# Two transformer blocks in float32 on one core: the low halves of the weights prepared first and multiplied last, and four smaller edits

## The chip, the core and the metric

The kernel runs on one core of a Trainium2 chip. The core has a matrix engine (TensorE, "PE" in the profile, with its weight loads as "PEld"), a vector engine (DVE), a scalar engine (ACT), GpSimd (POOL) and SyncE (SP). Each engine works through its own instructions in their fixed order and waits on semaphores; transfers are issued by SP, ACT or POOL and run on 16 DMA engines. The metric is the device time of one execution in microseconds (us). The three runs shown took 2757.64, 2758.91 and 2762.56 us, so the median is 2758.91 us; the profiled execution took 2760.67 us.

## The reference

Two networks of two layers each run one after the other over 512 tokens of width 1024, all in float32. A layer of the first one, cut to what matters here:

```
h = rmsnorm(x, g_mix)
dq, dk, dv, c_q, c_kv_kr, xq, gate_logits = split(h @ w_in)
y_diff = diff_attention(dq, dk, dv, ...) @ w_diff_o      # 8 heads, two softmax maps a head
y_mla  = latent_attention(c_q, c_kv_kr, ...) @ w_mla_o   # 8 heads
mem_n  = rmsnorm(mem, mem_gain)
y_mem  = memory_cross_attention(xq, mem_n, w_mem_kv) @ w_cross_o   # 4 heads, 256 memory rows
merged = gates[0]*y_diff + gates[1]*y_mla + gates[2]*y_mem
x = x + merged @ w_out
x = x + square(relu(rmsnorm(x, g_mlp) @ w_mlp1)) @ w_mlp2
```

In `diff_attention` a head's output is `o = softmax0 @ v - lam * softmax1 @ v`, and then `o = rmsnorm(o, out_gain)` times a constant. A layer of the second network projects with `w_in_2`, mixes by four branches (two of them causal attention), and adds the product with `w_out_2`.

## The kernel before, in words

Activations lie in SBUF with features or tokens on the 128 partitions and 512 (or 256) columns beside them. A float32 product is made from three products of a shorter format: every operand is split into a high half (rounded to `float32r`) and a low half (the rest), and `mm3` (line 206) adds high x high, high x low and low x high in PSUM. For weights, `W[0]` (tile `whi`) is the high half and `W[1]` (tile `wlo`) the low one.

Weights stream through a ring. `load` (line 120) takes one unit's weights, mostly 128 x 2048 values (1 MB): SP fetches them from HBM into `wraw`, then the halves are made. `whi`, `wlo` and `wraw` have two buffers each. For the first two loads the low half is a subtraction. For all later ones ACT casts `whi` (line 135, pieces of 1216 and 832 columns), ACT writes the negated raw weights into `wlo` (line 144), and POOL issues a transfer (line 147) that adds `wraw` onto `wlo` as it moves.

The work is cut into units, each with a generator that issues its products in parts. `run` (line 176) goes through the list `ops`; when a unit is begun, the load of the next unit is recorded. That load needs the `whi` and `wlo` buffers of the unit before, so its casts can begin when PE has read that unit's last weights. From the order of recording, the tile framework makes a fixed order for each engine.

`proj_tok` (line 477) makes a tile of tokens (activations stationary, weights moving), `proj_feat` (line 484) a tile of features (weights stationary). Both call `mm3` for k = 0 to 7, so high and low products alternate. An MLP unit (`w1`, `w2`, lines 1348 and 1370) is two feature tiles of 24 products of 512 columns.

`diff_chain` (line 642) is one head of the differential attention: `T` transposes q and k, `soft` makes both softmax maps of a block of queries and joins them, `pt` transposes the probabilities, `AV` multiplies by v, `sums` adds squares over features on PE (`tok_sums`, line 435) and takes 1/sqrt (`rsqrt`, line 221: two integer steps and three Newton rounds of three, 11 small operations of DVE), and `fin` spreads the root by a copy on DVE and four transposes on PE (`bcast`, line 447; line 453), and scales the output. `mla_chain` (line 930) does the same for the latent attention. `cross` (line 986) makes the memory's keys (`kk`, line 1024) and values (`vv`) in four units of 48 products of 256 columns. `layer1` (line 1171) weaves chains and units.

Of the kernel before, what the change touches and what calls it, by code (L numbers as in the profile page):

```python
# [20 lines left out]
TB = 4  # L21
# [63 lines left out]
class Net:  # L85
# [34 lines left out]
    def load(self, spec):  # L120
# [12 lines left out]
        for a in range(0, sz, 1216):  # L133
            b = min(a + 1216, sz)
            nc.scalar.copy(hi[:, a:b], raw[:, a:b])  # L135
        if self.loaded < 2:
            e, step = (nc.gpsimd, 576) if eng == "pool" else (nc.vector, 768)
            for a in range(0, sz, step):
                b = min(a + step, sz)
                e.tensor_tensor(lo[:, a:b], raw[:, a:b], hi[:, a:b].bitcast(F32), op=OP.subtract)  # L140
        else:
            for a in range(0, sz, 1216):
                b = min(a + 1216, sz)
                nc.scalar.activation(lo[:, a:b], raw[:, a:b], AF.Copy, scale=-1.0)  # L144
            for a in range(0, sz, 2048):
                b = min(a + 2048, sz)
                nc.gpsimd.dma_start(lo[:, a:b].bitcast(F32), raw[:, a:b], accum_op=OP.add)  # L147
        self.loaded += 1
# [72 lines left out]
    def rsqrt(self, t, shape, name):  # L221
        v = self.nc.vector
# [11 lines left out]
    def setup_x(self, gain):  # L234
# [12 lines left out]
        self.xt, self.gm = xt, gm  # L247
        self.consts = b.tile([128, NCONST], F32, name="consts")
# [186 lines left out]
    def tok_sums(self, sq, scale, name, more=()):  # L435
# [8 lines left out]
        nc.vector.tensor_scalar(t_, ps[:, 0:8:2], scale, EPS, op0=OP.mult, op1=OP.add)  # L444
# [32 lines left out]
    def proj_tok(self, out, W, tb, c0, c1, lh=None, ll=None):  # L477
        lh, ll = lh or self.hh, ll or self.hl
        n = len(lh)
        sl = slice(tb * 128, tb * 128 + 128)  # L480
        for k in range(n):
            self.mm3(out, lh[k][:, sl], ll[k][:, sl], W[0][:, k, c0:c1], W[1][:, k, c0:c1], k == 0, k == n - 1)

    def proj_feat(self, out, W, c0, rh, rl, order=None, m=128):
        n = len(rh)
        for i, k in enumerate(order or range(n)):
            self.mm3(out, W[0][:, k, c0:c0 + m], W[1][:, k, c0:c0 + m], rh[k], rl[k], i == 0, i == n - 1)
            if i == n // 2 - 1 and n == 8:
                yield
# [152 lines left out]
    def diff_chain(self, l, h):  # L642
        X = {}

        def T():
            p = self.pool("diff")
            t1s, X["f"] = self.t1s.pop(h)
            for i, nm in enumerate(("q", "k")):
                ps = self.P("tq")
                for tb in range(TB):  # L650
                    c = (tb % 2) * 256 + i * 128
                    self.nc.tensor.transpose(ps[:, tb * 128:(tb + 1) * 128], t1s[tb // 2][:, c:c + 128], self.ident)
                hi = p.tile([128, 512], F32R, name=nm + "h", bufs=1)
                lo = p.tile([128, 512], F32R, name=nm + "l", bufs=1)
                self.split(hi, lo, ps)
                X[nm] = (hi, lo)

        def soft(qb):
# [3 lines left out]
            sm = self.sm([128, 2], "dsm")  # L662
# [14 lines left out]
            rs = self.sm([128, 2], "drs")  # L677
            nc.vector.reciprocal(rs, sm)
            c = self.sm([128, 1], "dc")
            nc.vector.tensor_tensor(c, rs[:, 1:2], self.neglam[:, l:l + 1], op=OP.mult)  # L680
            nc.vector.tensor_scalar(Ss[0][:, :n], Ss[0][:, :n], rs[:, 0:1], None, op0=OP.mult)
# [17 lines left out]
        def sums():  # L699
            t = self.tok_sums(X["sq"], 1.0 / 128, "oss")  # L700
# [9 lines left out]
        return T, [lambda qb=qb: soft(qb) for qb in range(4)], [lambda qb=qb: pt(qb) for qb in range(4)], [AV, sums, fin]  # L710
# [219 lines left out]
    def mla_chain(self, l, h):  # L930
        X = {}

        def T():
            p = self.pool("mla2")
            for nm, src, g in (("k", self.kt, self.gqk_mla[l][0:96]), ("q", self.qt, None)):
                ps = self.P("tq")
# [1149 lines left out]
```

## Time and profile before

| what | us |
|---|---|
| median of the three runs | 2758.91 |
| profiled execution | 2760.67 |
| its span, first to last instruction | 2758.8 |
| PE busy in it | 2613.7 (95%) |
| ACT busy | 1560.8 (57%) |
| DVE busy | 1375.5 (50%) |
| POOL busy | 363.8 (13%) |

PE is the busy engine. "Busy" is the union of the records of an engine; records of neighbouring matmuls overlap, so the pace of PE is read from start to start. Idle time of PE, 145.1 us of the span, is what waits put there. The profile names for each wait what ended it, and the mean granted clock of PE (0.976 here) in parts of 2.4 GHz.

### The profile page before, as it was taken

What the parts mean: (1) busy time and instruction counts of PE and PEld (TensorE: products, weight loads), DVE (VectorE), ACT (ScalarE), POOL (GpSimd) and SP (SyncE); (2) the same over time, 40 slices, a digit from 0 to 9 for tenths busy, and PEclk for the clock granted to TensorE, in tenths of its full rate; (3) what the DMA queues carried; (4) which work ended last, traced back from release to release, by engine and by line L of the source; (5) the groups of instructions that cost most, each with busy time, mean ns of one, the idle gap of its engine ahead of it and who ended that gap; (6) DMA issues with size and microseconds to landing.
All of it is one profiled execution on the core that took longest, in us unless ns stands there. A gap on an engine that the chain in (4) does not pass through costs nothing.

```text
span 2758.8 us, 37849 instructions
## 1 busy us (share of the span) xinstructions
PE 2613.7 (95%) x14168; PEld 2199.3 (80%) x14168; DVE 1375.5 (50%) x4128; ACT 1560.8 (57%) x2699; POOL 363.8 (13%) x396
## 2 busy tenths in 40 slices
PE   7999998899999999999999799899999999999997
PEld 7998787787777778998788787677777978788776
DVE  6876575333201213777567342211113489728894
ACT  5666676454544445566667454444445557656683
POOL 1000200001100122000110000100031212121111
PEclk8999999899999999999999899999999999999999
DMA  6554745668777778555564666777777764475543
GB/s 194 123 134 100 176 119 128 160 157 211 177 177 185 184 180 210 138 133 121 123 151 108 168 168 164 191 180 183 187 180 203 176 138 111 119 184 120 146 108 99
DMA packets 261208, 428.83 MB, mean 155 GB/s; under 512 B 21724, under 2 KB 217120, under 8 KB 237728
## 3 DMA queue, kind: packets, MB, share of 16 engines
q0 software_dynamic: 29088, 199.14, 36.0%
q1 hardware_dynamic: 231224, 226.90, 26.8%
q8 instruction: 112, 1.84, 0.3%
q14 instruction: 72, 0.59, 0.1%
q10 hardware_dynamic: 712, 0.36, 0.0%
HBM read 216.76 MB, written 10.49 MB: 82 GB/s over the span
## 4 chain that ended last, share of the span: by engine, by line
PE 68%; DMA 14%; issue 7%; ACT 6%; DVE 5%; POOL 0%; SPq 0%; POOLq 0%; DVEq 0%; ACTq 0%
PE mm L210 18%; PE mm L208 18%; PE mm L209 18%; DMA wlo<-wraw 11%; PE tp L616 2%; PE sc L609 2%; ACT whi L135 2%; DMA wraw<-in_w_in 2%; PE av L632 1%; ACT wlo L144 1%; DMA wraw<-in_w_mem_kv 1%; PE sc L441 1%; PE av L208 1%; PE sc L210 1%; PE sc L208 1%
## 5 line engine op out<-in xcount | busy, mean ns | idle before, releaser
L135 ACT CAST whi<-wraw 128x1216 fp32r<-128x1216 f32 (+4 forms) x380 | 393.9, 1056 | 455.9 <-PE mm L209 390.5
L210 PE MATMUL mm<-hh,wlo 128*128 128x512 f32 x1312 | 526.4, 401 | 28.0 <-DMA wlo<-wraw 26.1
L208 PE MATMUL mm<-hh,whi 128*128 128x512 f32 x1312 | 528.3, 403 | 6.0 <-ACT hh L1999 4.6
L209 PE MATMUL mm<-hl,whi 128*128 128x512 f32 x1312 | 524.5, 400 | 0.0
L144 ACT ACTIVATE wlo<-wraw 128x1216 fp32r<-128x1216 f32 (+4 forms) x376 | 392.2, 1064 | 103.2 <-PE mm L209 66.3
L147 POOL DMA_DIRECT2D wlo<-wraw x202 | 176.4, 886 | 1970.1 <-ACT wlo L144 1610.4
L208 PE MATMUL mm<-whi,hh 128*128 128x256 f32 (+4 forms) x1184 | 349.2, 295 | 9.6 <-DVE xm L308 7.2
L209 PE MATMUL mm<-wlo,hh 128*128 128x256 f32 (+4 forms) x1184 | 343.6, 291 | 14.0 <-DMA wlo<-wraw 13.9
L210 PE MATMUL mm<-whi,hl 128*128 128x256 f32 (+4 forms) x1184 | 341.8, 289 | 0.0
L210 PEld LDWEIGHTS mm<-hh,wlo 128*128 128x128 f32 x1312 | 249.4, 190 | 93.5 <-issue 16.2
L208 PEld LDWEIGHTS mm<-hh,whi 128*128 128x128 f32 x1312 | 249.6, 190 | 59.5 <-ACT hh L1999 7.4
L209 PEld LDWEIGHTS mm<-hl,whi 128*128 128x128 f32 x1312 | 249.9, 190 | 52.3 <-DVE hl L2000 0.9
L209 PEld LDWEIGHTS mm<-wlo,hh 128*128 128x128 f32 x1184 | 228.8, 193 | 17.0 <-issue 8.1
L208 PEld LDWEIGHTS mm<-whi,hh 128*128 128x128 f32 x1184 | 228.4, 193 | 15.0 <-ACT hh L218 7.4
L210 PEld LDWEIGHTS mm<-whi,hl 128*128 128x128 f32 x1184 | 228.6, 193 | 0.0
L210 PE MATMUL mm<-sh,wlo 128*128 128x512 f32 x512 | 204.2, 399 | 6.2 <-DMA wlo<-wraw 5.4
L209 PE MATMUL mm<-sl,whi 128*128 128x512 f32 x512 | 202.5, 396 | 0.0
L208 PE MATMUL mm<-sh,whi 128*128 128x512 f32 x512 | 202.1, 395 | 0.0
L1360 DVE SCALAR_TENSOR_TENSOR sf<-mm,a 128x512 f32<-128x512 f32 x64 | 44.3, 692 | 311.4 <-ACT a L1358 311.4
L210 PEld LDWEIGHTS mm<-sh,wlo 128*128 128x128 f32 x512 | 96.1, 188 | 37.0 <-issue 5.4
L215 ACT CAST pth<-tp 128x128 fp32r<-128x128 f32 x224 | 91.7, 420 | 47.8 <-PE tp L616 47.3
L209 PEld LDWEIGHTS mm<-sl,whi 128*128 128x128 f32 x512 | 96.2, 188 | 23.4
(635 smaller groups left out, 4967.4 us busy)
## 6 DMA issues: line engine op xcount, KB each, us to landing
wlo<-wraw POOLq DMA_DIRECT2D x182, 1024.0 KB, 7.0
wraw<-in_w_mlp SPq DMA_DIRECT2D x64, 1024.0 KB
wraw<-in_w_in SPq DMA_DIRECT2D x54, 1024.0 KB
wraw<-in_w_in SPq DMA_DIRECT2D x36, 512.0 KB
wraw<-in_w_out SPq DMA_DIRECT2D x16, 1024.0 KB
xd<-xm SPq DMA_DIRECT2D x32, 256.0 KB
wraw<-in_w_diff_o SPq DMA_DIRECT2D x8, 1024.0 KB
wraw<-in_w_mem_kv SPq DMA_DIRECT2D x8, 1024.0 KB
```

The lines of the kernel that those rows point to most:

```text
L135: nc.scalar.copy(hi[:, a:b], raw[:, a:b])
L144: nc.scalar.activation(lo[:, a:b], raw[:, a:b], AF.Copy, scale=-1.0)
L147: nc.gpsimd.dma_start(lo[:, a:b].bitcast(F32), raw[:, a:b], accum_op=OP.add)
L208: mm(out, ah, bh, start=first, stop=False)
L209: mm(out, ah, bl, start=False, stop=False)
L210: mm(out, al, bh, start=False, stop=last)
L215: nc.scalar.copy(hi, src)
L441: nc.tensor.matmul(ps[:, 2 * t:2 * t + 2], q[:, t * 128:(t + 1) * 128], self.ones[:, 0:2], start=i == 0 and t == 0, stop=i == len(sqs) - 1 ...
L609: self.nc.tensor.matmul(pss[m][:, :n], q[a][sl, c], k[b][sl, :n], start=i == 0, stop=i == 2)
L616: self.nc.tensor.transpose(ps[:, kb * 128:(kb + 1) * 128], P[:, kb * 128:(kb + 1) * 128], self.ident)
L632: self.nc.tensor.matmul(out[:, s0 * 128:512], vs[kb], p[:, 3 * kb + s0:3 * kb + 4, :].rearrange("p b q -> p (b q)"), start=first and kb == ...
L1360: nc.vector.scalar_tensor_tensor(sf, ps, 0.0, a, op0=OP.max, op1=OP.mult)
```

## The change

1. In `load`, for all but the first two loads, the low half comes before the high one: the negated copy in two halves (split at `kt // 2`), each followed by its own adding transfer, and the casts of `whi` recorded after that. For units marked "dve" (the MLP, `w_out`, part of `w_out_2`) DVE makes the negated copy, for the others ACT as before.
2. `proj_tok` and `proj_feat` make all products with the high half of the weights first, then those with the low half. Other users of `mm3` (`wout`, `ckv`, attention) stay.
3. Roots of at most four values a partition are one power operation of POOL; wider ones stay on DVE.
4. `diff_chain`: the first map is no longer divided by its sum; the second is scaled by lam, its own sum's inverse and the first sum, and EPS is scaled by the square of the first sum, which gives the same output after the norm.
5. The transposes of q and k are two steps (`T[0]`, `T[1]`), woven apart.
6. `kk` copies the memory keys out of PSUM on ACT at once, and scales the copy.

```diff
@@ -130,21 +130,26 @@
         rv = raw[:, :sz].rearrange("p (k n) -> p k n", k=kt)
         for ap, c0, c1 in parts:
             nc.sync.dma_start(rv[:, :, c0:c1], ap.rearrange("(k p) n -> p k n", p=128))
-        for a in range(0, sz, 1216):
-            b = min(a + 1216, sz)
-            nc.scalar.copy(hi[:, a:b], raw[:, a:b])
+
+        def high():
+            for a in range(0, sz, 1216):
+                b = min(a + 1216, sz)
+                nc.scalar.copy(hi[:, a:b], raw[:, a:b])
         if self.loaded < 2:
+            high()
             e, step = (nc.gpsimd, 576) if eng == "pool" else (nc.vector, 768)
             for a in range(0, sz, step):
                 b = min(a + step, sz)
                 e.tensor_tensor(lo[:, a:b], raw[:, a:b], hi[:, a:b].bitcast(F32), op=OP.subtract)
         else:
-            for a in range(0, sz, 1216):
-                b = min(a + 1216, sz)
-                nc.scalar.activation(lo[:, a:b], raw[:, a:b], AF.Copy, scale=-1.0)
-            for a in range(0, sz, 2048):
-                b = min(a + 2048, sz)
+            cut = kt // 2 * n
+            for a, b in ((0, cut), (cut, sz)):
+                if eng == "pool":
+                    nc.scalar.activation(lo[:, a:b], raw[:, a:b], AF.Copy, scale=-1.0)
+                else:
+                    nc.vector.tensor_scalar(lo[:, a:b], raw[:, a:b], -1.0, None, op0=OP.mult)
                 nc.gpsimd.dma_start(lo[:, a:b].bitcast(F32), raw[:, a:b], accum_op=OP.add)
+            high()
         self.loaded += 1
         return (hi[:, :sz].rearrange("p (k n) -> p k n", k=kt),
                 lo[:, :sz].rearrange("p (k n) -> p k n", k=kt))
@@ -219,6 +224,16 @@
             nc.vector.scalar_tensor_tensor(lo, src, g, hi.bitcast(F32), op0=OP.mult, op1=OP.subtract)
     def rsqrt(self, t, shape, name):
+        if math.prod(shape[1:]) > 4:
+            return self.rsqrt_wide(t, shape, name)
+        y = self.sm(shape, name + "_y")
+        h = self.mhalf[0:shape[0]]
+        for _ in range(len(shape) - 2):
+            h = h[:, None]
+        self.nc.gpsimd.tensor_tensor(y, t, h.to_broadcast(shape), op=OP.pow)
+        return y
+
+    def rsqrt_wide(self, t, shape, name):
         v = self.nc.vector
         yi = self.sm(shape, name + "_i", I32)
         v.tensor_scalar(yi, t.bitcast(I32), 1, None, op0=OP.arith_shift_right)
@@ -245,6 +260,8 @@
...
+        self.mhalf = b.tile([128, 1], F32, name="mhalf")
+        nc.gpsimd.memset(self.mhalf, -0.5)
...
@@ -441,7 +458,10 @@
...
-        nc.vector.tensor_scalar(t_, ps[:, 0:8:2], scale, EPS, op0=OP.mult, op1=OP.add)
+        if eps is None:
+            nc.vector.tensor_scalar(t_, ps[:, 0:8:2], scale, EPS, op0=OP.mult, op1=OP.add)
+        else:
+            nc.vector.scalar_tensor_tensor(t_, ps[:, 0:8:2], scale, eps, op0=OP.mult, op1=OP.add)
...
@@ -478,14 +498,19 @@
         lh, ll = lh or self.hh, ll or self.hl
         n = len(lh)
         sl = slice(tb * 128, tb * 128 + 128)
+        mm = self.nc.tensor.matmul
         for k in range(n):
-            self.mm3(out, lh[k][:, sl], ll[k][:, sl], W[0][:, k, c0:c1], W[1][:, k, c0:c1], k == 0, k == n - 1)
+            mm(out, lh[k][:, sl], W[0][:, k, c0:c1], start=k == 0, stop=False)
+            mm(out, ll[k][:, sl], W[0][:, k, c0:c1], start=False, stop=False)
+        for k in range(n):
+            mm(out, lh[k][:, sl], W[1][:, k, c0:c1], start=False, stop=k == n - 1)
     def proj_feat(self, out, W, c0, rh, rl, order=None, m=128):
         n = len(rh)
-        for i, k in enumerate(order or range(n)):
-            self.mm3(out, W[0][:, k, c0:c0 + m], W[1][:, k, c0:c0 + m], rh[k], rl[k], i == 0, i == n - 1)
-            if i == n // 2 - 1 and n == 8:
+        ops = [(W[0], r, k) for k in range(n) for r in (rh, rl)] + [(W[1], rh, k) for k in range(n)]
+        for i, (w, r, k) in enumerate(ops):
+            self.nc.tensor.matmul(out, w[:, k, c0:c0 + m], r[k], start=i == 0, stop=i == 3 * n - 1)
+            if i == 11 and n == 8:
...
@@ -642,24 +667,25 @@
...
-        def T():
-            p = self.pool("diff")
-            t1s, X["f"] = self.t1s.pop(h)
-            for i, nm in enumerate(("q", "k")):
...
+        def T(i):
+            p, nm = self.pool("diff"), "qk"[i]
+            t1s, X["f"] = self.t1s[h]
+            ps = self.P("tq")
...
+            self.split(hi, lo, ps)
+            X[nm] = (hi, lo)
...
-            sm = self.sm([128, 2], "dsm")
+            if qb == 0:
+                X["sm"] = p.tile([128, TB, 2], F32, name="dsm", bufs=2)
+            sm = X["sm"][:, qb]
...
@@ -674,11 +700,10 @@
...
-            rs = self.sm([128, 2], "drs")
-            nc.vector.reciprocal(rs, sm)
+            rs = self.sm([128, 1], "drs")
+            nc.vector.reciprocal(rs, sm[:, 1:2])
             c = self.sm([128, 1], "dc")
-            nc.vector.tensor_tensor(c, rs[:, 1:2], self.neglam[:, l:l + 1], op=OP.mult)
-            nc.vector.tensor_scalar(Ss[0][:, :n], Ss[0][:, :n], rs[:, 0:1], None, op0=OP.mult)
+            nc.vector.scalar_tensor_tensor(c, rs, sm[:, 0:1], self.neglam[:, l:l + 1], op0=OP.mult, op1=OP.mult)
             nc.vector.scalar_tensor_tensor(Ss[0][:, :n], Ss[1][:, :n], c, Ss[0][:, :n], op0=OP.mult, op1=OP.add)
...
@@ -697,7 +722,10 @@
...
         def sums():
-            t = self.tok_sums(X["sq"], 1.0 / 128, "oss")
+            e = self.sm([128, TB], "oes")
+            s0 = X["sm"][:, :, 0]
+            self.nc.vector.scalar_tensor_tensor(e, s0, EPS, s0, op0=OP.mult, op1=OP.mult)
+            t = self.tok_sums(X["sq"], 1.0 / 128, "oss", eps=e)
             X["y"] = self.rsqrt(t, [128, TB], "or")
...
@@ -930,16 +958,16 @@
...
+        def T(nm):
             p = self.pool("mla2")
-            for nm, src, g in (("k", self.kt, self.gqk_mla[l][0:96]), ("q", self.qt, None)):
...
+            src, g = (self.kt, self.gqk_mla[l][0:96]) if nm == "k" else (self.qt, None)
+            ps = self.P("tq")
+            for tb in range(TB):
...
@@ -1031,6 +1059,8 @@
...
                 sq = p.tile([128, 512], F32, name="csq", bufs=2)
                 nc.scalar.activation(sq, ps, AF.Square)
+                kn = kn_[j] = p.tile([128, 512], F32, name="ckn", bufs=2)
+                nc.scalar.copy(kn, ps)
                 ss = self.sm([128, 2, 2], "cks")
...
@@ -1039,8 +1069,8 @@
...
-                kn = kn_[j] = p.tile([128, 512], F32, name="ckn", bufs=2)
-                nc.vector.tensor_tensor(kn.rearrange("p (g d) -> p g d", d=128), ps.rearrange("p (g d) -> p g d", d=128),
+                kv = kn.rearrange("p (g d) -> p g d", d=128)
+                nc.vector.tensor_tensor(kv, kv,
                                         y.rearrange("p t h -> p (t h)")[:, :, None].to_broadcast([128, 4, 128]), op=OP.mult)
...
@@ -1190,9 +1220,9 @@
...
-                chain = [T, pt[2], sf[0], pt[3], sf[1], tail[0], sf[2], tail[1], sf[3], tr[0], tail[2], tr[1]]
+                chain = [T[1], pt[2], T[0], pt[3], sf[0], sf[1], tail[0], sf[2], tail[1], sf[3], tr[0], tail[2], tr[1]]
             else:
-                chain = [T] + sf + tr[:2]
+                chain = T + sf + tr[:2]
...
@@ -1228,14 +1258,16 @@
...
-        self.plain(fill[:4], mc[0][0])
+        self.plain(fill[:2], mc[0][0][0], fill[2:4], mc[0][0][1])
...
             T, sf, tr, nxt = mc[h]
-            chain = [sf[0]] + ([pt[2]] if pt else []) + [sf[1]] + ([pt[3]] if pt else []) + sf[2:] + ([av] if av else [])
-            chain += tr[:1] + ([mc[h + 1][0]] if h < 7 else []) + tr[1:2]
+            nk = mc[h + 1][0] if h < 7 else [None, None]
+            chain = [sf[0]] + ([pt[2]] if pt else []) + [sf[1]] + ([pt[3]] if pt else []) + sf[2:]
+            chain += [nk[0], av, tr[0], nk[1], tr[1]]
+            chain = [c for c in chain if c]
...
```

The order of the instructions before and after, at three places. The first is PE at the first `w2` unit of the first layer's MLP (`sh`, `sl`: the activations' halves; `hh7`, `hl7`: those of the unit before). Before, from the last three products of the unit before on:

```order
L208 MATMUL mm_7987<-hh7_7402,whi_7871 128x512
L209 MATMUL mm_7987<-hl7_7410,whi_7871 128x512
L210 MATMUL mm_7987<-hh7_7402,wlo_7872 128x512
L208 MATMUL mm_8029<-sh_7739,whi_7946 128x512
L209 MATMUL mm_8029<-sl_7740,whi_7946 128x512
L210 MATMUL mm_8029<-sh_7739,wlo_7947 128x512
L208 MATMUL mm_8029<-sh_7772,whi_7946 128x512
```

Now, from the thirteenth product of that unit's first tile on:

```order
L512 MATMUL mm_7897<-sh_7850,whi_7812 128x512
L512 MATMUL mm_7897<-sl_7851,whi_7812 128x512
L512 MATMUL mm_7897<-sh_7883,whi_7812 128x512
L512 MATMUL mm_7897<-sl_7884,whi_7812 128x512
L512 MATMUL mm_7897<-sh_7603,wlo_7813 128x512
L512 MATMUL mm_7897<-sh_7636,wlo_7813 128x512
L512 MATMUL mm_7897<-sh_7679,wlo_7813 128x512
```

A unit's first product with `wlo` was its third; it is its seventeenth now.

The second place is ACT beside the same units (`acc`: the copy of a finished `w2` tile). Before:

```order
L1386 COPY acc0_8054<-mm_8029 128x512
L135 CAST whi_8084<-wraw_8083 128x1216
L1386 COPY acc1_8081<-mm_8056 128x512
L135 CAST whi_8084<-wraw_8083 128x832
L144 ACTIVATE wlo_8085<-wraw_8083 128x1216
L144 ACTIVATE wlo_8085<-wraw_8083 128x832
```

Now:

```order
L1418 COPY acc0_7922<-mm_7897 128x512
L137 CAST whi_7952<-wraw_7951 128x1216
L137 CAST whi_7952<-wraw_7951 128x832
L1418 COPY acc1_7949<-mm_7924 128x512
L1418 COPY acc2_7986<-mm_7961 128x512
L137 CAST whi_8016<-wraw_8015 128x1216
```

The two operations on `wlo` have left ACT; they stand on DVE (line 150).

The third place is DVE at the root of a head's norm in the differential attention (`oss`: the mean square plus EPS, `or_i`, `or_b`: the root's steps, `oa`: the copy that spreads it for PE). Before, the first ten rows; the copy `oa` comes 17 rows further down:

```order
L444 TENSOR_SCALAR oss_2059<-sc_2054 128x4
L682 SCALAR_TENSOR_TENSOR Sa_2012<-Sb_2014,dc_2022,Sa_2012 128x384
L224 TENSOR_SCALAR or_i_2061<-oss_2059 128x4
L668 ISA Sa_2084,dmx_2074<-sc_2076,mask_244 128x512
L668 ISA dmx_2074 128x1
L219 SCALAR_TENSOR_TENSOR vl_1884<-mm_1977,r_tok_408,vh_1883 128x256
L225 TENSOR_SCALAR or_i_2061<-or_i_2061 128x4
L668 ISA Sb_2086,dmx_2074<-sc_2077,mask_244 128x512
L668 ISA dmx_2074 128x1
L229 TENSOR_TENSOR or_b_2064<-or_i_2061 128x4
```

Now (`or_y` is POOL's result):

```order
L464 SCALAR_TENSOR_TENSOR oss_2015<-sc_2010,oes_2008 128x4
L707 SCALAR_TENSOR_TENSOR Sa_1967<-Sb_1969,dc_1977,Sa_1967 128x384
L470 COPY oa_2045<-or_y_2017 128x512
L694 ISA Sa_2028,dmx_2019<-sc_2020,mask_246 128x512
L694 ISA dmx_2019 128x1
L224 SCALAR_TENSOR_TENSOR vl_1842<-mm_1933,r_tok_399,vh_1841 128x256
```

The copy has moved up to the third row, and it waits for POOL there, with the next block's scores (`L694`) queued behind it.

## Rows read from the trace of the kernel before

**Rows 1.** The page, busy time, share of the span and instructions by engine:

```profile
PE 2613.7 (95%) x14168; PEld 2199.3 (80%) x14168; DVE 1375.5 (50%) x4128; ACT 1560.8 (57%) x2699; POOL 363.8 (13%) x396
```

**Rows 2.** PE's waits, whole span: total us, times, longest us:

```profile
PE mm L209 <- DMA wlo<-wraw: 39.0, 12, 5.2
PE mm L210 <- DMA wlo<-wraw: 35.6, 39, 7.1
...
PE mm L208 <- DVE ckn L1043: 6.7, 2, 4.4
```

**Rows 3.** The windows view: length, PE, PEld, DVE, ACT, POOL busy, PEclk, DMA, GB/s:

```profile
450.00:502.00 52.00, 33.93 (x224) 32.02 (x223) 15.70 (x59) 25.21 (x34) 4.31 (x5) 0.80 0.70 171
...
660.00:1065.00 405.00, 390.42 (x1672) 311.05 (x1671) 81.93 (x120) 192.50 (x241) 62.53 (x60) 1.00 0.74 185
```

**Rows 4.** PE's waits within 450 to 502 and within 660 to 1065 us:

```profile
PE mm L209 <- DMA wlo<-wraw: 12.4, 3, 5.2
...
PE mm L210 <- DMA wlo<-wraw: 13.8, 16, 2.4
```

**Rows 5.** Timelines of ACT, POOL, PE at one MLP unit: start, length, [idle before]:

```profile
795.88 1.21 ACT L135 CAST whi<-wraw 128x1216 fp32r<-128x1216 f32 x1 [4.83 <-PE mm L209]
...
798.26 2.00 ACT L144 ACTIVATE wlo<-wraw 128x1216 fp32r<-128x1216 f32 x2
...
800.66 0.86 POOL L147 DMA_DIRECT2D wlo<-wraw  x1 [10.53 <-ACT wlo L144]
...
807.09 0.39 PE L208 MATMUL mm<-hh,whi 128*128 128x512 f32 x1
807.32 0.40 PE L209 MATMUL mm<-hl,whi 128*128 128x512 f32 x1
809.42 0.50 PE L210 MATMUL mm<-hh,wlo 128*128 128x512 f32 x1 [1.71 <-DMA wlo<-wraw]
```

**Rows 6.** The DMA view, low-half transfers: KB each, median us to landing:

```profile
wlo<-wraw POOLq DMA_DIRECT2D x182, 1024.0 KB, 7.0
...
wlo<-wraw POOLq DMA_DIRECT2D x8, 576.0 KB, 4.9
```

**Rows 7.** Groups by form: busy us, mean ns of one, idle before:

```profile
L144 ACT ACTIVATE wlo<-wraw 128x1024 fp32r<-128x1024 f32 x4 | 4.2, 1062 | 4.2 <-PE mm L209 4.2
...
L681 DVE TENSOR_SCALAR Sa<-Sa,drs 128x512 f32<-128x512 f32 x16 | 7.7, 480 | 0.0
...
L681 DVE TENSOR_SCALAR Sa<-Sa,drs 128x128 f32<-128x128 f32 x16 | 4.5, 281 | 0.0
```

**Rows 8.** The chain that ended last, in the memory units: start, us, what:

```profile
455.61 6.93 DMA wlo<-wraw
462.61 12.40 DMA wraw<-in_w_mem_kv
```

**Rows 9.** The windows view, ten stretches of half clock; the first, and all:

```profile
310.40:317.20 6.80, 5.16 (x12) 4.11 (x13) 0.81 (x2) 2.69 (x7) 0.89 (x1) 0.50 0.69 157
...
sum 74.80, PE 50.78 PEld 46.84 DVE 13.13 ACT 30.54 POOL 12.53; mean PE 5.08 PEld 4.68 DVE 1.31 ACT 3.05 POOL 1.25
```

**Rows 10.** A head's root in the timelines of PE and DVE:

```profile
149.10 0.95 PE L441 MATMUL sc<-ones,oa 128*128 128x2 f32 x8
...
156.59 0.42 DVE L450 COPY oa<-or_i 128x512 f32<-128x512 f32 x1
...
157.07 0.66 PE L453 MATMUL sc<-ident,oa 128*128 128x128 f32 x4
```

**Rows 11.** Groups by form, small operations of DVE, and POOL's own:

```profile
L231 DVE SCALAR_TENSOR_TENSOR or_i<-or_b,or_i 128x4 f32<-128x4 f32 x48 | 7.6, 159 | 0.8
...
L433 POOL TENSOR_TENSOR sqa<-sqa,sqx 128x512 f32<-128x512 f32 x41 | 54.3, 1323 | 174.7 <-ACT sqx L429 174.7
...
L923 POOL TENSOR_TENSOR qt<-qr,qr 128x128 f32<-128x128 f32 x16 | 7.7, 481 | 13.0 <-DVE qr L922 9.4 <-DVE ckr_b L229 3.2 <-DVE mkt L885 0.5
```

More of the change, by code (lines that the diff above doesn't have):

```diff
@@ L433, in norm_tile, with tok_sums @@
                 nc.gpsimd.tensor_tensor(self.sqa, self.sqa, sq, op=OP.add)
-    def tok_sums(self, sq, scale, name, more=()):
+    def tok_sums(self, sq, scale, name, more=(), eps=None):
         nc = self.nc
@@ L643, in diff_chain @@
         X = {}
-        def T():
-            p = self.pool("diff")
-            t1s, X["f"] = self.t1s.pop(h)
-            for i, nm in enumerate(("q", "k")):
[L649 to L656, printed above, removed]
+        def T(i):
[3 more added lines that the diff above has]
+            for tb in range(TB):
+                c = (tb % 2) * 256 + i * 128
+                self.nc.tensor.transpose(ps[:, tb * 128:(tb + 1) * 128], t1s[tb // 2][:, c:c + 128], self.ident)
+            hi = p.tile([128, 512], F32R, name=nm + "h", bufs=1)
+            lo = p.tile([128, 512], F32R, name=nm + "l", bufs=1)
+            self.split(hi, lo, ps)
+            X[nm] = (hi, lo)
         def soft(qb):
@@ L708, in fin @@
             self.new_o(o)
-        return T, [lambda qb=qb: soft(qb) for qb in range(4)], [lambda qb=qb: pt(qb) for qb in range(4)], [AV, sums, fin]
+        return [lambda: T(0), lambda: T(1)], [lambda qb=qb: soft(qb) for qb in range(4)], [lambda qb=qb: pt(qb) for qb in range(4)], [AV, sums, fin]
     def new_o(self, src):
@@ L931, in mla_chain @@
         X = {}
-        def T():
+        def T(nm):
             p = self.pool("mla2")
-            for nm, src, g in (("k", self.kt, self.gqk_mla[l][0:96]), ("q", self.qt, None)):
-                ps = self.P("tq")
-                for tb in range(TB):
-                    self.nc.tensor.transpose(ps[0:96, tb * 128:(tb + 1) * 128], src[:, tb, h, :], self.ident)
-                hi = p.tile([128, 512], F32R, name="m" + nm + "h", bufs=1)
-                lo = p.tile([128, 512], F32R, name="m" + nm + "l", bufs=1)
-                self.split(hi[0:96], lo[0:96], ps[0:96], g)
-                X[nm] = (hi, lo)
+            src, g = (self.kt, self.gqk_mla[l][0:96]) if nm == "k" else (self.qt, None)
+            ps = self.P("tq")
+            for tb in range(TB):
+                self.nc.tensor.transpose(ps[0:96, tb * 128:(tb + 1) * 128], src[:, tb, h, :], self.ident)
+            hi = p.tile([128, 512], F32R, name="m" + nm + "h", bufs=1)
+            lo = p.tile([128, 512], F32R, name="m" + nm + "l", bufs=1)
+            self.split(hi[0:96], lo[0:96], ps[0:96], g)
+            X[nm] = (hi, lo)
         def soft(qb):
@@ L977, in AV @@
                 self.o.append(self.mo)
-        return T, [lambda qb=qb: soft(qb) for qb in range(4)], [lambda qb=qb: pt(qb) for qb in range(4)], AV
+        return [lambda: T("k"), lambda: T("q")], [lambda qb=qb: soft(qb) for qb in range(4)], [lambda qb=qb: pt(qb) for qb in range(4)], AV
     def mem_load(self):
```

## The prediction

> **What bounds the kernel now.** I read the engines' busy times first, then PE's waits over the whole span, then the same waits by stage, then the timeline of one unit, and last the stretches of half clock. PE is busy for 2613.7 of 2758.8 us [rows 1]: it sets the time, and only what shortens its work or its waits counts. The change leaves PE's work alone: the same 14028 products stand in the new order, in another sequence. So the idle 145.1 us and the stretches of low clock are all there is to win.
>
> One cause holds half of the idle time. PE waits for the adding transfer of a low half 12 times as `L209` (`proj_tok`) and 39 times as `L210`, together 39.0 + 35.6 = **74.6 us** [rows 2]. A wait for the memory's keys in PSUM adds 6.7 [rows 2]. By stage, the four memory units of layer 1 wait 12.4 us in a window of 52, in which PE is busy for 33.9 at 0.80 of the clock; the MLP of layer 1 waits 13.8 us, 16 times, at full clock [rows 3, 4].
>
> The timeline shows why [rows 5]. A load's first cast begins at 795.88, when PE has read the last weights of an older unit. `whi` is cast, then `wlo` negated until 800.26, POOL issues at 800.66, and the low half is there at 809.42, **13.5 us** after the start. A unit is 48 products of 0.233 us from start to start (807.32 − 807.09), 11.2 us. The next unit's third product needs the low half 0.47 us after those 11.2: it waits 1.71.
>
> When PE waits, its clock falls afterwards: ten stretches run at 0.50 (1.2 GHz), six in the memory units of both layers, four elsewhere. PE is busy for 50.78 us in them [rows 9]; the same work at 2.4 GHz takes half, so they cost 25.4 us, 2.54 each.
>
> **The change part by part.** *MLP.* The first half's copy goes to DVE. DVE's scaling copies take 480 ns for 512 columns and 281 for 128 [rows 7], 0.52 ns a column, so an estimate of 0.75 us for 1024. With the 0.4 from copy to issue [rows 5] and 4.9 us, the landing of 576 KB, the nearest row to 512 [rows 6], the first half is there 6.1 us after the start. If the halves share the engines fully, both land at 7.0 + 0.75 + 0.4 = 8.2 or, one after the other, later by the copy and issue of the second. The first product with `wlo` is now the seventeenth: it needs its half at 11.2 + 16 × 0.233 = 14.9, the second half four products later. Slack is 6 us or more. The 13.8 us go. The casts of `whi` are now recorded last, but ACT no longer makes the copies, so they start as early as before. Two copies of 0.75 us a unit for DVE are covered: it is busy for 82 of the 405 us [rows 3].
>
> *All other low waits but the memory's.* The memory units of layer 2 are the same code; I take 12.4 for them too. One wait of 7.1, the longest of `L210` [rows 2], is the second network's `w_out`, whose weights come late from HBM. 74.6 − 24.8 − 13.8 − 7.1 = 28.9 us stand in `kvb`, the second MLP and the other projections. Their low product moves from second or third to seventeenth too; `ckv` stays interleaved, and units on ACT gain less. I keep 5 and take 24.
>
> *`w_out`.* `wout` keeps `mm3`, so the wait shrinks but doesn't go. Before, the transfer waits for two casts and two copies; the casts' 1.21 + 0.85 us go, and DVE's copy of one half is shorter than ACT's 2.0: between 3.4 and 5.3 us, depending on whether the transfer of half the size is shorter as well. I take 4.2.
>
> *Memory units.* Here low transfer, raw buffer and HBM fetch form a ring: the chain of waits runs from a low transfer of 6.93 into a fetch of 12.40 [rows 8], since the fetch needs the buffer that the transfer reads. The casts of `whi` (2.06 us) leave this ring, and the first half starts 1.06 us earlier, as the second half's copy (1062 ns [rows 7]) isn't waited for: 3.1 us a load, four loads a layer. The fetch of 12.4 stays, and PE has only 33.9 us of work in the 52 [rows 3]. Of 31.5 us of waits in both layers (24.8 and the 6.7 for `ckn`, which the early copy on ACT removes at the price of one ACT operation) I keep 18 and take 13. Of six half-clock stretches (15.2 us) I take back 9. That is 11 a layer, under the 12.4 of the ring.
>
> *The other four stretches* cost 10.2; without the waits ahead of them I take back 8.
>
> *Roots.* Eleven operations of DVE at 159 ns [rows 11] give way to one of POOL. In the trace `sums` ends at 150.05, the copy for `fin` stands at 156.59 and PE's transposes at 157.07, without a wait [rows 10]. In the new order only some 1.6 us of PE's own work (2.9 at a few heads) stand between `sums` and those transposes. What must fit: the mean square on DVE (159 ns), the root, the copy (0.42 us [rows 10]). POOL's cost of a power is in no row. Its nearest operations take 481 ns for 128 columns and 1323 for 512 [rows 11]; a root has four columns, so I take less than the first for size and something above for the function, about 0.8 us with handing over. Up to two issues of 0.86 us [rows 5] may stand ahead on POOL, whose issues double (388 for 202, 160 us more of POOL, over a busy 363.8 [rows 1]). DVE waits at the copy meanwhile, with the next block's scores behind it. I take 0.3 us a head (0 to 1.6), 16 heads: **+5**. Undercutting zero is excluded, as no wait stands there now.
>
> *The rest*: the second copies, the split `T`, the saved scaling of the first map (480 ns on DVE) lie beside PE, which is busy throughout the attention stages; if that cover went, they cost some tenths a head. Nothing.
>
> Sum: 13.8 + 24 + 4.2 + 13 + 9 + 8 = 72 removed, 5 added. The profiled execution took 2760.67: 2760.67 − 67 = 2693.7. It lies 1.8 above the median of 2758.91, so I forecast **2692**.
>
> **The rivals.** *The halves go one after the other.* From 576 to 1024 KB the landing grows by 2.1 us [rows 6], 4.8 for a whole MB, which leaves 2.2 that is paid by every transfer. Paid twice, the raw buffer is released 2.2 later, and of the 3.1 us per memory load 0.9 stay. The MLP's slack bears it; of the 22 us of the memory units (13 + 9) 6 are left: 2692 + 16 = **2708**. The second half's copy does run beside the first transfer, but the transfer's fixed part might too, which speaks against. The Trainium skill has a rule that points this way: "DMA: Bandwidth & Descriptors", section "Anatomy of one DMA — SWDGE (gpsimd) path", gives about 2.0 us fixed for each such transfer, and the bytes at 436 GB/s beside it. By it a half would take an estimated 3.2 us and a whole 4.4, less than the 7.0 of the row, and splitting costs 2.0; the fixed part agrees with the rows' 2.2, the rate doesn't.
>
> *The fetch from HBM takes the place of the low wait.* DMA is busy for 0.74 in the MLP [rows 3]; a faster chain asks for more, and a fetch of 12.4 is longer than a unit's 11.2 us. If so, the MLP keeps its 13.8 and half of the 24 stays: 2692 + 26 = **2718**. Against it: two raw buffers give a fetch more than one unit, and PE already runs at 390 of the 405 us, so the rate asked rises by 4% only.
>
> *The root comes late, and the kernel is slower.* If POOL answers after more than the gap, every head waits at its transposes and the scores behind. The gap holds 0.6 us beside the mean square and the copy; the 72 us are used up at 72 / 16 = 4.5 us a head, so it decides from a root of 5.1 us on, issues ahead included. At 6 us: 16 × 5.4 = 86, instead of the 5: **2773**. For it: the power has no row, and two issues may stand ahead. Against: POOL's longest row here is 1323 ns for 128 times the columns. The Trainium skill, "SBUF — State Buffer", section "Who interferes with whom", says that DVE in some operations locks a port that it shares with GpSimd, which then stands still for the whole instruction. No row of before shows this for a root; with it one DVE operation of some 0.5 us would be added, well under the 5.1.
>
> *It doesn't do what it says.* The casts of `whi` are now last in each load; where ACT makes all (the memory, the attention's units) they come later than before by the copies' 2.1 us, and PE's first product waits for them instead. If this and the roots cancel the gain in full: about **2757**.
>
> **How the numbers follow.** The forecast has .68, the halves one by one .10, the fetch .11, the late root .05, no gain .06. The forecast's own bounds: all low waits and all clock go and nothing is added, 74.6 + 6.7 + 25.4 = 107, which gives 2652; I end at 2655, as the ring can't vanish. Upward, the range takes in 1.6 us for each of 16 heads (+21 → 2713) and both milder rivals: 2722. No gain and the late root are left out. About 0.2%, 5.5 us, is what a measurement can tell from no change. Faster: .68 + .10 + .11 = .89; same .06; slower .05.
>
> **What the profile of after would show.** The waits for `wlo<-wraw` down from 74.6 to 20 to 30 us, none in the MLP from 660 to 1065; adding transfers of 512 KB at 4.9 to 7 us; the memory window shorter by some 11 us, with the fetch `wraw<-in_w_mem_kv` as its main wait; half-clock stretches down from ten to four or five; at the fin transposes a new wait for DVE's copy of 0 to 1.6 us a head, and POOL's root under 1 us. I am wrong if low waits stay above 45 us, if PE waits instead for `whi` or raw weights, or if the waits at fin pass 25 us together.

## The result, and the profile after

The changed kernel took 2694.2 us (median of four runs, 2690.85 to 2704.03) against 2760.7 for the kernel before: a ratio of 0.977, 95% interval 0.974 to 0.979. Forecast were 2692 and a range of 2655 to 2722. The span of the profiled execution fell from 2758.8 to 2690.8 us, by 68.0.

The page of the changed kernel, busy time by engine, answers to [rows 1]:

```profile
PE 2573.5 (96%) x14168; PEld 2183.9 (81%) x14168; DVE 1434.6 (53%) x3891; ACT 1423.0 (53%) x2563; POOL 565.7 (21%) x614
```

PE is busy for 40 us less with the same instructions, so not all of the gain is idle time. PE's waits over the whole span (total us, times, longest) answer to [rows 2]:

```profile
PE mm L506 <- DMA wlo<-wraw: 17.7, 8, 5.2
PE sc L213 <- ACT xqh L220: 12.2, 2, 6.2
PE sc L473 <- DVE dmx L694: 11.1, 12, 1.4
...
PE mm L215 <- DMA wlo<-wraw: 5.8, 2, 5.6
```

The waits for low halves went from 74.6 to 23.5 us. Two large waits, for `xqh` and `dmx`, are new. The windows view (length, PE, PEld, DVE, ACT, POOL busy, PEclk, DMA, GB/s) of the memory units and of the first MLP answers to [rows 3]:

```profile
446.00:487.00 41.00, 30.24 (x229) 29.32 (x227) 11.13 (x34) 21.93 (x30) 9.16 (x10) 0.88 0.83 181
653.00:1059.00 406.00, 403.15 (x1796) 330.40 (x1795) 133.07 (x198) 137.84 (x183) 110.44 (x113) 1.00 0.81 195
```

The memory window is shorter. Its clock of 0.88 instead of 0.80 owes much to where it ends: a stretch of half clock runs from 484.06 to 494.30 us, and from 446 to 495 us the mean is 0.83. In the MLP PE now hardly waits. One load there, in the timeline of ACT, DVE and POOL (start, length, [idle before]), answers to [rows 5]:

```profile
782.80 2.00 ACT L137 CAST whi<-wraw 128x1216 fp32r<-128x1216 f32 x2 [3.12 <-PE mm L512]
784.59 1.30 DVE L150 TENSOR_SCALAR wlo<-wraw 128x1024 fp32r<-128x1024 f32 x2 [9.69 <-PE mm L512]
785.70 1.76 POOL L151 DMA_DIRECT2D wlo<-wraw  x2 [9.23 <-DVE wlo L150]
```

DVE copies two halves in 1.30 us beside ACT's casts, and POOL issues two transfers. DVE starts 1.8 us after ACT: `wlo` is now read by the last products of a unit, so its buffer comes free later than that of `whi`. The two halves landed at 790.67 and 793.15, 7.9 and 10.4 us after the first cast's start; before it was 13.5.

The stretches of half clock, one row and the sum of all (length, PE busy, ...), first of the kernel before with its 19 stretches, then of the changed one with its 16. In each kernel the last holds no product:

```profile
481.10:491.34 10.24, 5.63 (x23) 5.00 (x24) 2.73 (x7) 5.88 (x9) 0.88 (x1) 0.50 0.79 181
...
sum 136.23, PE 92.67 PEld 81.22 DVE 48.71 ACT 58.39 POOL 24.89; mean PE 4.88 PEld 4.27 DVE 2.56 ACT 3.07 POOL 1.31
```

```profile
484.06:494.30 10.24, 6.02 (x28) 6.03 (x29) 3.36 (x7) 6.30 (x11) 1.72 (x2) 0.50 0.75 183
...
sum 82.51, PE 59.53 PEld 53.67 DVE 29.88 ACT 43.17 POOL 14.83; mean PE 3.72 PEld 3.35 DVE 1.87 ACT 2.70 POOL 0.93
```

PE is busy for 33.1 us less at 1.2 GHz; half of that, an estimated 16.6 us, is time won. The ten stretches of the prediction [rows 9] are only part of the 19.

### The profile page after: what moved, and what is told of

It is laid out like the page before. It is cut to its first block, busy times and chain, and to the rows that moved or that the text cites. A ratio compares the mean times of both kernels' runs of the same rounds, so it can differ in the third digit from the quotient of the medians.

```text
span 2690.8 us, 37953 instructions
## 1 busy us (share of the span) xinstructions
PE 2573.5 (96%) x14168; PEld 2183.9 (81%) x14168; DVE 1434.6 (53%) x3891; ACT 1423.0 (53%) x2563; POOL 565.7 (21%) x614
## 4 chain that ended last, share of the span: by engine, by line
PE 39%; DVE 4%; DMA 4%; ACT 3%; issue 2%; POOL 1%; POOLq 0%; DVEq 0%; SPq 0%; ACTq 0%
PE mm L512 24%; DMA wraw<-in_w_in 2%; PE mm L506 1%; PE mm L503 1%; PE mm L504 1%; PE mm L213 1%; PE mm L215 1%; PE mm L214 1%; DMA wlo<-wraw 1%; PE av L657 1%; PE tp L641 1%; ACT wlo L148 1%; ACT whi L137 1%; PE sc L1517 0%; PE sc L1518 0%
## 5 line engine op out<-in xcount | busy, mean ns | idle before, releaser
L151 POOL DMA_DIRECT2D wlo<-wraw x388 | 346.2, 943 | 1628.1 <-ACT wlo L148 886.8
L503 PE MATMUL mm<-whi,hh 128*128 128x256 f32 (+3 forms) x1152 | 298.0, 294 | 14.2 <-DVE xm L325 7.3
L512 PE MATMUL mm<-hh,wlo 128*128 128x512 f32 x1216 | 311.5, 394 | 0.0
L504 PE MATMUL mm<-whi,hl 128*128 128x256 f32 (+3 forms) x1152 | 291.3, 288 | 0.3 <-DVE hl L224 0.3
L512 PEld LDWEIGHTS mm<-hl,whi 128*128 128x128 f32 x1216 | 229.9, 189 | 45.3
L148 ACT ACTIVATE wlo<-wraw 128x1024 fp32r<-128x1024 f32 (+6 forms) x236 | 237.2, 1027 | 18.4 <-DMA wraw<-in_w_mem_kv 9.0
L150 DVE TENSOR_SCALAR wlo<-wraw 128x1024 fp32r<-128x1024 f32 x152 | 107.7, 746 | 177.0 <-PE mm L512 160.7
L506 PE MATMUL mm<-wlo,hh 128*128 128x256 f32 (+3 forms) x1152 | 168.8, 288 | 0.0
L506 PEld LDWEIGHTS mm<-wlo,hh 128*128 128x128 f32 x1152 | 152.4, 192 | 0.5 <-issue 0.5
L512 PE MATMUL mm<-sh,wlo 128*128 128x512 f32 x512 | 127.8, 392 | 0.0
L221 DVE TENSOR_TENSOR ptl<-tp,pth 128x128 fp32r<-128x128 f32 x224 | 106.6, 482 | 16.8 <-ACT pth L220 15.5
```

The costliest lines, as they stand in the source:

```text
L150: nc.vector.tensor_scalar(lo[:, a:b], raw[:, a:b], -1.0, None, op0=OP.mult)
L221: nc.vector.tensor_tensor(lo, src, hi.bitcast(F32), op=OP.subtract)
L503: mm(out, lh[k][:, sl], W[0][:, k, c0:c1], start=k == 0, stop=False)
L504: mm(out, ll[k][:, sl], W[0][:, k, c0:c1], start=False, stop=False)
L506: mm(out, lh[k][:, sl], W[1][:, k, c0:c1], start=False, stop=k == n - 1)
L512: self.nc.tensor.matmul(out, w[:, k, c0:c0 + m], r[k], start=i == 0, stop=i == 3 * n - 1)
```

## The experiments

Each was timed in three rounds beside the kernel before, on one chip a group. Ratios are to the kernel before, which took 2756.3 to 2760.7 us in the groups; so where two kernels of different groups are compared, the ratios say more than the medians.

| kernel | us | ratio, 95% interval |
|---|---|---|
| the changed kernel | 2694.2 | 0.977 (0.974 to 0.979) |
| load_only | 2682.8 | 0.972 (0.970 to 0.974) |
| load_one | 2679.1 | 0.973 (0.971 to 0.975) |
| order_only | 2702.7 | 0.979 (0.978 to 0.981) |
| order_undone | 2698.6 | 0.978 (0.976 to 0.980) |
| one_transfer | 2680.8 | 0.972 (0.969 to 0.974) |
| roots_dve | 2690.4 | 0.974 (0.972 to 0.977) |
| roots_dve_fix | 2679.4 | 0.972 (0.971 to 0.974) |
| roots_dve_one | 2666.3 | 0.968 (0.966 to 0.970) |
| t_whole | 2692.5 | 0.976 (0.974 to 0.978) |
| no_early_keys | 2694.5 | 0.978 (0.976 to 0.979) |
| shift_96 | 2705.6 | 0.980 (0.979 to 0.982) |
| aligned | 2695.6 | 0.977 (0.976 to 0.979) |

**load_only and order_only: each half of the main edit alone.** The first is the kernel before with the hunk of `load` alone, the second with the products' new order alone:

```diff
-            self.mm3(out, lh[k][:, sl], ll[k][:, sl], W[0][:, k, c0:c1], W[1][:, k, c0:c1], k == 0, k == n - 1)
+            mm(out, lh[k][:, sl], W[0][:, k, c0:c1], start=k == 0, stop=False)
...
+            mm(out, lh[k][:, sl], W[1][:, k, c0:c1], start=False, stop=k == n - 1)
...
```

> The kernel before with the new order of work in load alone (low half first, in two transfers, DVE or ACT for the negated copy); the products alternate as before, roots, T and keys are as before. Theory: in the MLP the earlier transfer is enough by itself, since the first half is there 6 to 8 us after the unit's start and the third product of the next unit needs it after 11.7; the waits for low halves from 660 to 1065 vanish, all of them together fall from 74.6 to about 25 us, and the time is 2695 to 2710. Rival: what pays is that the low products come last; then the low waits stay above 45 us and the time above 2725.

> The kernel before with the new order of products alone (high products first, low ones last in each tile); load, roots, T and keys are as before. Theory: in the MLP this too is enough by itself, as the low half came after 13.5 us and would be needed after 14.9; the memory units, whose ring of transfers isn't shortened, keep most of their waits and half-clock stretches. Low waits 30 to 45 us, the time 2710 to 2725. Rival: the order alone does as much as both, 2700 or less; or it does nothing without the earlier transfer, above 2745.

Measured 2682.8 and 2702.7: both below what was expected, and `load_only` is below the changed kernel, its interval touching that kernel's at 0.974. PE's waits for the low halves, whole span, of `load_only`, then of `order_only`:

```profile
PE mm L213 <- DMA wlo<-wraw: 32.0, 18, 5.0
...
PE mm L214 <- DMA wlo<-wraw: 6.4, 3, 5.0
```

```profile
PE mm L486 <- DMA wlo<-wraw: 18.4, 11, 3.1
...
PE mm L210 <- DMA wlo<-wraw: 16.2, 6, 8.2
...
PE mm L492 <- DMA wlo<-wraw: 3.2, 6, 1.3
```

38 us of the 74.6 are left in each, where `load_only` was expected to keep 25. In the MLP from 660 to 1040 us each has next to none (0.7 and 0.8 us): there an earlier transfer or a later need is enough, as expected. Both together bring the waits to 23.5, but the time doesn't follow. So the rest of the change must cost something. The traces show where: `load_only` has neither of the two new waits (23.3 us), PE is idle in it for 98.2 us where it is for 117.3 in the changed kernel, and busy at 1.2 GHz for 43.0 us instead of 59.5; against that stand 15 us more of low waits and the slower pace of 512-column products that comes up below.

**order_undone.** The changed kernel with the products alternating again:

> The changed kernel with high and low products alternating again in both projections; all else as changed. Theory, since the earlier transfer alone was enough: the new order adds nothing, 2688 to 2697. Rival of the prediction's sum: the order carries part of the gain beside the transfer; low waits rise by 10 us or more and the time to 2702 or above.

Measured 2698.6, 4.4 above the changed kernel with overlapping intervals. Low waits are 36.6 instead of 23.5. Neither theory is clean: the order does take 13 us of waits away, and the time shows a third of it at most.

**roots_dve, then roots_dve_fix.** All roots on DVE again:

```diff
     def rsqrt(self, t, shape, name):
-        if math.prod(shape[1:]) > 4:
-            return self.rsqrt_wide(t, shape, name)
...
+        return self.rsqrt_wide(t, shape, name)
```

> The changed kernel with every root on DVE again (eleven small operations), all else as changed. Theory: the 11 us that PE waits at the transposes of fin (12 waits in the trace of after, 16 heads) are due to the root on POOL, which takes 1.27 us; they vanish and the time falls by 8 to 11 us against the changed kernel, to 2683 to 2687. Rival: the small operations on DVE delay other work by as much, and the time stays at 2692 to 2696.

Measured 2690.4, between theory and rival. The wait at `fin` was gone, and PE's 512-column products had become slower: 233 ns from start to start in the first layer's `w2` units, where the changed kernel has 229. The larger root tiles had moved later tiles by some bytes. The second kernel adds two unused tiles (128 and 192 bytes) that put them back:

```diff
-        net.open("small")
+        net.open("small").tile([128, 32], F32, name="spad")
...
-                self.open("small")
+                self.open("small").tile([128, 48], F32, name="spad")
```

> As roots_dve (every root on DVE again), with two unused tiles that bring sh, sl, oh, ol and mt back to the distance 192 from the weights, which the larger root tiles had moved off it. Theory: the root on POOL costs 11 us at fin, and roots_dve showed only 4 of them since the layout took 7 back; here the time is 2681 to 2686. Rival: the layout has no part in it, and the time stays at 2688 to 2694.

Measured 2679.4, 14.8 below the changed kernel in medians, **12** by the ratios, whose intervals don't overlap. The timeline of the changed kernel at a root shows what it costs:

```profile
145.13 1.27 POOL L233 TENSOR_TENSOR or_y<-oss,mhalf 128x4 f32<-128x4 f32 x1 [12.46 <-DVE oss L464]
...
146.44 0.43 DVE L470 COPY oa<-or_y 128x512 f32<-128x512 f32 x1 [0.93 <-POOL or_y L233]
...
146.78 0.68 DVE L694 CUSTOM_DVE_ANT_0 Sa<-sc,mask 128x512 f32<-128x512 f32 x1
...
147.53 0.66 PE L473 MATMUL sc<-ident,oa 128*128 128x128 f32 x4 [0.72 <-DVE dmx L694]
```

POOL takes 1.27 us for four columns; DVE stands idle for 0.93 us at the copy; the scores (`L694`) queue behind it; PE's transposes wait 0.72 us, by the profile for those scores. Before, the copy stood 6.5 us behind the sums and PE didn't wait [rows 10].

**shift_96 and aligned: the pace of PE by address.** The first moves all tiles behind the small ones by 96 bytes, the second moves the second weight ring and the second layer's MLP tiles by 128:

```diff
-        net.open("small")
+        net.open("small").tile([128, 24], F32, name="spad")
...
```

> The changed kernel with an unused tile of 96 bytes a partition ahead of the small tiles, so that all later tiles lie 96 bytes further; same instructions in the same order. Theory: what sets the pace of 512-column products is how the moving tile's address stands to that of the weights: where they differ by 192 modulo 256 a product takes 229.4 ns in all kernels so far, at other distances 233; the shift moves sh, sl, oh, ol and mt off it, some 2500 products at 4 ns, and the time rises by 8 to 11 us against the changed kernel, with 233 ns in the second half of each MLP. Rival: the pace comes from elsewhere (what runs beside PE), and nothing moves by more than 3 us.

> The changed kernel with two unused tiles of 128 bytes, one ahead of the second weight ring and one ahead of the second layer's MLP tiles; same instructions. Theory of addresses: hh and hl in the second layer's MLP and in the second network come to the distance 192 as well, 1500 products at 4 ns, mx leaves a good one (220 products): 4 to 6 us faster than the changed kernel, 229 ns through the second MLP. Rival: no move.

`shift_96` took 2705.6, 11.4 above the changed kernel (10.5 by the ratios, whose intervals meet at 0.979). The pace follows the address in every trace. From start to start at the full clock, 512-column products of the tile `mm` that could be matched with the addresses in the compiled program (waits left out), by the difference of the weights' (stationary) and the moving tile's address modulo 256. Some 220 products in each kernel have the difference 0; they took 229.2 to 230.6 ns and are in neither column:

| kernel | at 192: products, ns | elsewhere: products, ns |
|---|---|---|
| before | 2030, 229.9 | 4090, 233.5 |
| load_only | 2060, 229.5 | 4197, 233.5 |
| changed | 4461, 229.4 | 1760, 233.2 |
| roots_dve | 2156, 229.5 | 4054, 233.1 |
| shift_96 | 2066, 230.2 | 4169, 233.9 |
| aligned | 6160, 229.4 | 42, 233.1 |

In the windows view (PE's count is the first in brackets) one 30 us stretch of `w2` in the second layer, of the changed kernel and then of `shift_96`:

```profile
1795.00:1825.00 30.00, 30.00 (x133) 24.61 (x132) 3.70 (x6) 9.20 (x12) 3.52 (x5) 1.00 0.81 192
```

```profile
1803.00:1833.00 30.00, 30.00 (x130) 24.11 (x129) 2.96 (x5) 8.92 (x12) 3.51 (x4) 1.00 0.79 183
```

Same clock, same products, 133 against 130. `aligned` brought nearly all products to 229.4 ns, and yet its time stayed at 2695.6, as its rival said. From 1750 to 2050 us its waits have what those of the changed kernel don't:

```profile
ACT whi L137 <- DMA wraw<-in_w_mlp: 28.1, 6, 6.3
...
DVE wlo L150 <- DMA wraw<-in_w_mlp: 23.6, 4, 11.1
...
PE mm L512 <- ACT sh L220: 4.4, 2, 2.3
```

As I read these lines, with PE a little faster the fetch from HBM comes late; ACT stands at a cast for the next unit, and `sh`, which PE needs, is queued behind it. So the pace is shown to follow the address; that the time follows is shown for `shift_96` alone.

**one_transfer, load_one, roots_dve_one: halves or a whole.**

```diff
-            cut = kt // 2 * n
-            for a, b in ((0, cut), (cut, sz)):
+            for a, b in [(a, min(a + 2048, sz)) for a in range(0, sz, 2048)]:
```

> The changed kernel with one negated copy and one adding transfer a load instead of two halves (a second only beyond 2048 columns, as before the change); all else as changed. Theory: the MLP's slack of some 5 us covers the later landing; where the ring of transfers is the limit (memory units) each load comes about 1 us later, eight loads: 2696 to 2704. Rival: a fixed part paid by each transfer makes two halves dearer, and one transfer is better by 5 us or more: below 2690.

> The kernel before with one edit: the low half is made first in each load, by DVE or ACT, with one adding transfer; order of products, roots, T and keys are as before. Theory: the order inside load is what pays, and halves cost some 10 us: 2670 to 2678. Rival: alternating products need the early half of the low weights; low waits rise above 50 us and the time to 2690 or more.

> As roots_dve_fix, and one adding transfer a load instead of two halves. If the two savings add (13 us of one_transfer, 10 of the roots): 2668 to 2674. If the fetch of weights from HBM bounds the rest: 2675 to 2681.

`one_transfer` took 2680.8: halves cost the changed kernel **13.4** us (14 by the ratios), in the direction of the rival. With roots on DVE it is 13.0 again (2679.4 to 2666.3); `load_one`, whose products alternate, has the same ratio as `load_only` (its 2679.1 lies just above the 2678 expected), so there halves cost nothing that shows. Landings of low transfers in the DMA view of the changed kernel and of `one_transfer`:

```profile
wlo<-wraw POOLq DMA_DIRECT2D x348, 512.0 KB, 5.8
```

```profile
wlo<-wraw POOLq DMA_DIRECT2D x182, 1024.0 KB, 7.2
```

Over all loads, the second half lands 7.7 us (median) after the first was issued, the whole 7.1: a loss of 0.6, not the 2.2 of the rival. By the rule of the Trainium skill ("DMA: Bandwidth & Descriptors", "Anatomy of one DMA — SWDGE (gpsimd) path"; 2.0 us fixed each) the loss would be an estimated 2.0; the measurement decides, and the halves overlap. What the halves do is double the entries in the queues, and with them the fixed order changes. In `one_transfer` low waits are higher (26.2 + 6.8), but this wait of the changed kernel, 12.2 us there, is nearly gone:

```profile
PE sc L212 <- ACT xqh L219: 0.6, 1, 0.6
```

In the changed kernel ACT stands at a cast for a later load, with `xqh` behind it:

```profile
486.17 1.20 ACT L137 CAST whi<-wraw 128x1216 fp32r<-128x1216 f32 x1 [8.25 <-DMA wraw<-in_w_in]
...
487.65 0.57 ACT L220 CAST xqh<-tq 128x512 fp32r<-128x512 f32 x1
```

In `one_transfer` the first operation of that later load stands behind `xqh`:

```profile
484.41 0.59 ACT L219 CAST xqh<-tq 128x512 fp32r<-128x512 f32 x1
484.89 1.92 ACT L147 ACTIVATE wlo<-wraw 128x2048 fp32r<-128x2048 f32 x1
```

The spans of the two traces differ by 10.4 us; PE is idle for 6.9 us less (117.3 to 110.4), and busy at 1.2 GHz for 45.7 us instead of 59.5. By landmarks in PE's order (the same product in both traces), one transfer makes the memory units 1.7 and 3.1 us shorter in the two layers and the attention ahead of them 1.4 and 2.7; from the memory to the end of the MLP it is 2.0 shorter in the first layer and 2.0 longer in the second. For the memory units the `xqh` wait is the reason, part of it given back in low waits; for the other stages I have no line that shows why.

**roots_dve_one beats both kernels**: 2666.3 us, 28 below the changed one (25 by the ratios), and a little below the 2668 to 2674 expected. The two savings add.

**t_whole and no_early_keys.** The transposes as one step again, and the keys scaled out of PSUM by DVE again:

```diff
-                chain = [T[1], pt[2], T[0], pt[3], sf[0], sf[1], tail[0], sf[2], tail[1], sf[3], tr[0], tail[2], tr[1]]
+                chain = [lambda T=T: (T[0](), T[1]()), pt[2], sf[0], pt[3], sf[1], tail[0], sf[2], tail[1], sf[3], tr[0], tail[2], tr[1]]
...
```

```diff
-                kn = kn_[j] = p.tile([128, 512], F32, name="ckn", bufs=2)
-                nc.scalar.copy(kn, ps)
...
+                nc.vector.tensor_tensor(kn.rearrange("p (g d) -> p g d", d=128), ps.rearrange("p (g d) -> p g d", d=128),
```

> The changed kernel with the transposes of q and k as one step again, at the place they had before. Theory: the split costs PE a little in the latent attention, where the changed kernel is 2 to 4 us a layer longer than those without the split: 2687 to 2692. Rival: the split hides waits, and without it the time is 2697 or more.

> The changed kernel without the early copy of the memory keys: DVE scales them out of PSUM as before. Theory: PE's wait for the keys in PSUM comes back, 4 to 7 us in two layers, 2697 to 2702. Rival: the wait moves to another place of the memory units, whose end is set by the fetch of the weights, and the time stays at 2691 to 2696.

2692.5, just outside the theory's range, and 2694.5, as the rival said: neither differs from the changed kernel. Without the early keys their wait comes back as one of 2.1 us; it had been 6.7 [rows 2] beside the longer low waits.

## Why the prediction was right, and where only its total was

| term | predicted, us | found, us |
|---|---|---|
| waits in the first MLP | −13.8 | −13.5 |
| other low waits | −24 | −23.3 |
| `w_out` | −4.2 | −1.5 |
| memory waits | −13 | −7.3 |
| half clock | −17 | −16.6 |
| roots | +5 | +11.1 in waits, +12 by the run's ratio |
| pace by address | none | −9 to −11 |

With the waits for `whi`, which fell from 4.2 to 0.7 and weren't in the sum, the terms found (11.1 for the roots, 9.4 for the pace) give −64 for a span that fell by 68.0. Two larger differences stand behind that: PE's idle time fell by 27.8 us (145.1 to 117.3) where the waits of the table give 38, so some 10 us of other, small waits are new; and its busy time fell by 40.2 where clock and pace give 26, so 14 us of it aren't accounted for.

**Right**: the cause, and the two large terms on low waits. The timeline [rows 5] gave the chain, and the MLP's waits vanished. 20 to 30 us of low waits were forecast to stay, and 23.5 did. The memory rows gave 22 us with their clock; the stretch from memory products to `w_out` shrank by 13.0 us in layer 1 and 7.7 in layer 2 (landmarks in PE's order), 20.7 in all, of which an estimated 1.5 are pace. One place was misread: the wait of 7.1 us stands at 1742 us in the second layer of the first network, not in the second network; its term is the same.

**Right in its total by luck: the clock.** The prediction took ten stretches for all; there are 18 in which PE works, and by the same estimate they cost 46.3 us, not 25.4. In the six of the memory units 3.9 us came back of the 9 forecast, in the other four some 3 of 8. The remaining 9.5 came from stretches that weren't in the sum. Not ten stretches became four or five, but 18 became 15.

**Mis-sized: the roots.** I took 0.8 us for POOL's power and 0.3 a head. It took 1.0 to 1.7 us, mean 1.21, 2.5 times the 481 ns row that I had put it beside and over the 1 us that I had expected to see, and PE waited 0.7 to 1.4 us at 12 of 16 heads. The range of 0 to 1.6 held it. The rival (slower from 5.1 us on) was far off.

**Mis-sized: `w_out`.** The 4.2 us let the first half land an estimated 6.2 us after its issue: the whole one's 7.0, less the 0.8 by which 4.2 exceeds 3.4. It was issued at 1690.15 and landed at 1698.10, 8 us later, with the second half behind it, and PE waited this long:

```profile
1698.15 0.79 PE L215 MATMUL mm<-hh,wlo 128*128 128x512 f32 x1 [5.56 <-DMA wlo<-wraw]
```

**Mis-sized: the memory.** The low waits there fell from 24.5 to 11.7 and the keys' 6.7 went, but 12.2 came back as the wait for `xqh`. I had named the fetch of the memory's weights as the next limit; it was that of `w_in`, and I didn't see that ACT would carry it to PE. This comes near one of my signs of being wrong, that PE waits for raw weights instead.

**Missed: the pace.** Smaller root tiles moved other tiles to better addresses, some 2400 products at 3.9 ns, an estimated 9.4 us; moving tiles off these addresses cost 11.4 (10.5 by the ratios). Nothing in the profile of before, read by groups, says so; its `w1` and `w2` units do differ by 4 ns a product, which I didn't ask about.

So 2692 against 2694 is partly chance: too little for the roots and too much gain for the memory and `w_out` on one side, and a missing gain on the other, cancel. **The rivals**: halves one by one were dearer by 13 us than one transfer, near the 16 of that rival, by another mechanism than its; the fetch from HBM did take over in the MLP, but only in `aligned`.

**Open**: the single undoings don't add up to `load_only`: from 2694.2, −14.8 (roots), +4.4 (order), −1.7 (T) and +11.4 (addresses) give 2693.5, and 2682.8 was measured. The halves weren't undone in `load_only`, so they are not in this sum. Edits of the order interact with the fixed queues, and the new form of the two softmax maps wasn't tried alone.

## What to carry to other kernels

Where an earlier supply or a later need would each remove a wait, time them apart: here the earlier supply alone gave at least as much as the whole change (0.972 against 0.977, the intervals just touching). A short chain moved to an idle engine is no gain if its consumer is then placed right behind it; compare the length of one operation there with the distance to who needs it. When a change alters how many operations stand in a queue, look at what now stands ahead of the operation that the busy engine waits for. Count the stretches of low clock over the whole span. And when a change adds or shrinks a tile, compare the pace of the same products in both traces, as addresses move with it.

## What was not expected of the hardware

A product of 512 columns took 229.4 to 230.2 ns (means) from start to start where the addresses of weights and moving tile differed by 192 modulo 256 bytes, 229.2 to 230.6 at 0, and 232 to 235 at 32, 64, 96, 128, 160 and 224, at the same granted clock, in the traces of the table. Why is open. POOL's power took 1.0 to 1.7 us for four columns, more than the 481 ns of its row for 128 columns [rows 11], and 0.72 for two:

```profile
L233 POOL TENSOR_TENSOR or_y<-oss,mhalf x16: 1032/1154/1668, 92.3 to 1310.8; 128x4 f32<-128x4 f32 x16
...
L233 POOL TENSOR_TENSOR memr_y<-memtt,mhalf x2: 716/716/717, 440.1 to 1471.0; 128x2 f32<-128x2 f32 x2
```

These rows give the shortest, median and longest in ns, the first and last start, and the shape.
